# Attention with scores seven tiles ahead of the transposes instead of five, and weighted sums one behind instead of three

## The chip, the cores and the metric

The kernel runs on one core of a Trainium2 chip. The metric is the device time of one execution in microseconds (us), as the median of several runs. Profiles come from the hardware profiler, one execution each. Engines: PE multiplies matrices (PEld loads its weights), DVE is the vector engine, ACT evaluates functions and copies, POOL is the general engine, SP issues DMA transfers.

## The reference

One layer on a sequence of 2048 positions and a width of 1024: an input projection feeds two groups of eight heads of 64, an RWKV-7 recurrence and a stick-breaking attention; both are gated, put side by side, projected out and normalised. The change touches only the attention:

```
z      = q @ k.T / 8                        # 2048 x 2048 per head, strictly causal
log_1m = where(mask, log_sigmoid(-z), 0)
after  = cumsum from the right of log_1m, without the own element
attn   = where(mask, exp(log_sigmoid(z) + after), 0)
o      = attn @ v
```

So each weight is sigmoid(z) times the product of sigmoid(-z) over all later keys that are still before the query.

## The kernel before, in words

The program is one function, `trunk`. A first stage (0 to 132 us in the profile) makes the modulated input and its two half-precision parts; attention follows (132 to 1033 us); a second stage, with its own planner context, holds the recurrence and the output projection. The change is in the attention alone.

**Blocks and steps.** Attention goes through 16 blocks n = 4 j + b: four head pairs j, and in each four blocks of 512 queries b. Block b has 8 (b + 1) steps, so 8, 16, 24 and 32, in all 320; `seq` (L484 to L486) lists them. A step i of a block has three jobs, and i means another thing in each:

- `scores` (L495 to L526), for one tile of 128 queries and 512 keys: two matmuls into the PSUM tile `z` (L506, L507); ACT writes `u` = sigmoid(-z/8) (L510) and `s` = sigmoid(z/8) (L511); DVE runs a product scan over `u` from the last key to the first (L519 on the diagonal, L522 elsewhere), which starts from a column that POOL copies from the neighbouring tile (L521); POOL multiplies `s` by the scanned `u` (L523). Diagonal tiles are 128, 256, 384 and 512 wide. A group is four such tiles, for the four query tiles of one head and one block of keys.
- `turn` (L528 to L541), for 128 keys of a group: four PE transposes (L535), one from each `s` tile of the group, into the PSUM tile `tr`; ACT rounds it into `ah` (L539); DVE writes the rest `al` = tr - ah (L540).
- `weigh` (L543 to L566): two matmuls of `ah` and `al` with the values into the PSUM tile `av` (L553, L554); at the end of a head the result is copied out (L563, L564) and after the second head normalised and stored to DRAM (`finish`, L568).

**What is written down as order.** `attend` (L587 to L605) emits the jobs. Four constants rule it:

```
NS, NU, LEAD, LAG = 8, 5, 5, 3                                              # L481
...
        for p in range(p0, p1):
            if p + LEAD < min(p1 + ahead, len(seq)):
                yield scores(*seq[p + LEAD], sb)
            held.append(turn(*seq[p], sb))
            yield 0.43
            if len(held) > LAG:
                weigh(sb, *held.pop(0))
            yield 0.43
```

`ahead` is LEAD, but 0 in the blocks of 8 steps, whose successors' queries are not ready; the blocks of 16 steps begin with LEAD scores on their own (L592 to L594). `NS` and `NU` are the numbers of buffers of `s` and `u` (L508, L509), and LAG + 1 is that of `ah` and of `al` (L537, L538). `tr` has two PSUM buffers, `z` three, the projections' accumulator one and `av` one (L113, L127). `u` is also the buffer of a tile in the last projections of attention (L644).

**What fills the rest.** `fill` (L647) emits projections for later blocks, the splitting of weights into two half-precision parts and the combining of earlier results; a projection is 24 matmuls of 128x512 (L370 to L372). `_merge` (L712) interleaves `attend` and `fill` by shares of work.

**What sets the executed order.** The attention stage is planned with a timeline (`schedule_with_timeline_sim`, L109). The order of emission is a rank: the planner goes through a modelled time and gives each engine the instruction of highest rank whose inputs and buffers are ready. The order it ends with is fixed at compile time, and each engine then executes it in order, with semaphores between engines. In the last four blocks the first matmul of each accumulation of a projection is also held behind the newest weighted sum emitted so far (`pace`, L369, L555).

Of the kernel before, what the change touches and what calls it, by code (L numbers as in the profile page):

```python
# [88 lines left out]
def trunk(nc, a, out):  # L89
# [388 lines left out]
        V.scalar_tensor_tensor(out=sg, in0=tp, scalar=vec("sbg", 1, j), in1=sg, op0=ALU.mult, op1=ALU.mult)  # L478
        DMA.dma_start(out=ydram[4 + j][b], in_=sg)

    NS, NU, LEAD, LAG = 8, 5, 5, 3  # L481


    seq, steps = [], {}  # L484
# [851 lines left out]
```

## Time and profile before

| | |
|---|---|
| median of three runs (lowest to highest) | 1914.78 us (1912.62 to 1915.76) |
| the profiled execution's own time | 1910.53 us |
| its span in the trace | 1908.8 us |
| mean granted PE clock | 0.971 |
| attention, in the trace | 132 to 1033 us |

The profiled execution took 4.25 us less than the median of the three runs and 2.09 less than the lowest. Its span, the time between the first and the last instruction of the trace, is 1.7 us shorter than its time. "Busy" is time in which an engine worked; a bracket behind an instruction in a timeline is the engine's idle time before it and what ended it. A granted clock of 1.00 is 2.4 GHz, 0.50 is 1.2 GHz.

### The profile page before, as it was taken

How to read it: one execution, taken by the hardware profiler on the slowest of the kernel's cores; microseconds unless marked ns; L12 is line 12 of the kernel's file. 1: busy time of each engine (PE TensorE's matmuls, PEld its weight loads, DVE VectorE, ACT ScalarE, POOL GpSimd, SP SyncE). 2: the span in 40 equal slices, each digit the busy share in tenths (PEclk: the TensorE clock that was granted, in tenths of full speed). 3: DMA queues.
4: the chain of work that ended last, by engine and by line, in shares of the span. 5: the costliest groups of instructions: out<-in, count | busy, mean ns of one | idle time of the engine just before them, and what ended most of it. 6: DMA issues, size and time to landing. Idle time of an engine off the chain costs nothing. (4 is left out here: it accounts for less than half of the span.)

```text
span 1908.8 us, 38922 instructions
## 1 busy us (share of the span) xinstructions
PE 1719.8 (90%) x14880; PEld 1161.5 (61%) x14880; DVE 1348.7 (71%) x2855; ACT 870.0 (46%) x1718; POOL 754.6 (40%) x1106
## 2 busy tenths in 40 slices
PE   7979889999899998999997898898899888989998
PEld 2646556666566665667654455665555565667886
DVE  4876788577776778768775667877877777775542
ACT  2665567366654656546654333323332333422221
POOL 1425466355643646445444223222223232223322
PEclk9889999999999999999998899999999999999999
DMA  8442201222123221132111423222333333236442
GB/s 298 150 116 56 56 26 50 64 64 70 37 56 81 67 56 42 51 92 67 45 50 56 133 55 83 68 60 74 77 81 81 80 77 107 75 94 179 149 138 89
DMA packets 210408, 159.93 MB, mean 84 GB/s; under 512 B 113247, under 2 KB 171820, under 8 KB 210222
## 3 DMA queue, kind: packets, MB, share of 16 engines
q1 hardware_dynamic: 209220, 155.31, 29.2%
q8 instruction: 117, 1.92, 0.4%
q10 hardware_dynamic: 1002, 2.13, 0.4%
q14 instruction: 69, 0.57, 0.1%
HBM read 94.48 MB, written 44.04 MB: 73 GB/s over the span
## 5 line engine op out<-in xcount | busy, mean ns | idle before, releaser
L523 POOL TENSOR_TENSOR s<-s,u 128x512 f32<-128x512 f32 (+2 forms) x320 | 305.8, 963 | 216.5 <-ACT s L511 102.0
L540 DVE TENSOR_TENSOR al<-tr,ah 128x512 fp32r<-128x512 f32 (+1 forms) x320 | 187.4, 599 | 96.3 <-ACT ah L539 95.7
L522 DVE TENSOR_TENSOR_SCAN u<-u,dmask 128x512 f32<-128x512 f32 x192 | 240.0, 1268 | 13.0 <-ACT u L510 11.4
L539 ACT ACTIVATE ah<-tr 128x512 fp32r<-128x512 f32 (+1 forms) x320 | 171.7, 553 | 103.7 <-PE tr L535 99.6
L510 ACT ACTIVATE u<-z 128x512 f32<-128x512 f32 (+2 forms) x320 | 173.4, 555 | 73.4 <-PE z L507 49.0
L535 PE MATMUL tr<-kept_ident,s 128*128 128x128 f32 x1088 | 173.5, 279 | 33.1 <-DVE al L540 26.5
L511 ACT ACTIVATE s<-z 128x512 f32<-128x512 f32 (+2 forms) x320 | 166.2, 549 | 53.0 <-PE tr L535 53.0
L535 PEld LDWEIGHTS tr<-kept_ident,s 128*128 128x128 f32 x1088 | 130.3, 143 | 74.9 <-DVE al L540 38.4
L370 PE MATMUL pss<-kept_hh,kept_wh 128*128 128x512 f16 x416 | 161.3, 388 | 8.8 <-PEq L730 8.8
L372 PE MATMUL pss<-kept_hh,kept_wl 128*128 128x512 f16 x416 | 160.9, 387 | 0.0
L371 PE MATMUL pss<-kept_hl,kept_wh 128*128 128x512 f16 x416 | 160.9, 387 | 0.0
L372 PEld LDWEIGHTS <-kept_wl 128*128 128x128 f16 x928 | 93.2, 100 | 104.9 <-issue 14.2
L370 PEld LDWEIGHTS <-kept_wh 128*128 128x128 f16 x928 | 94.3, 102 | 101.4 <-issue 29.2
L371 PEld LDWEIGHTS <-kept_wh 128*128 128x128 f16 x928 | 93.0, 100 | 94.8 <-issue 25.0
L506 PE MATMUL z<-kt,qt 128*128 128x512 f32 (+2 forms) x320 | 132.1, 417 | 9.5 <-issue 3.7
L553 PE MATMUL av<-ah,vt 128*128 128x512 f32 (+1 forms) x320 | 136.5, 427 | 3.9 <-DVE o L564 2.3
L554 PE MATMUL av<-al,vt 128*128 128x512 f32 (+1 forms) x320 | 136.0, 426 | 0.2 <-DVE al L540 0.2
L507 PE MATMUL z<-kt,qt 128*128 128x512 f32 (+2 forms) x320 | 117.5, 371 | 0.0
L519 DVE TENSOR_TENSOR_SCAN u<-u,dmask 128x128 f32<-128x128 f32 (+3 forms) x128 | 107.3, 867 | 11.6 <-ACT u L510 6.6
L370 PE MATMUL psg<-kept_hh,kept_wh 128*128 128x512 f16 x256 | 99.1, 387 | 10.9 <-DVE klo L434 4.8
L1274 PE MATMUL po<-kept_woh,kept_yh 128*128 128x512 f32 x256 | 102.3, 400 | 0.0
L1275 PE MATMUL po<-kept_wol,kept_yh 128*128 128x512 f32 x256 | 101.5, 397 | 0.0
(296 smaller groups left out, 4146.1 us busy)
## 6 DMA issues: line engine op xcount, KB each, us to landing
kept_raw<-in_w_in SPq DMA_DIRECT2D x29, 512.0 KB, 4.3
ad<-in_ada_w SPq DMA_DIRECT2D x24, 512.0 KB, 5.6
qt<-qt SPq DMA_DIRECT2D x48, 256.0 KB, 3.3
xt<-in_x SPq DMA_DIRECT2D x16, 512.0 KB, 5.1
y<-sg SPq DMA_DIRECT2D x32, 256.0 KB, 2.3
t<-dt SPq DMA_DIRECT2D x64, 128.0 KB, 3.2
xr<-in_x SPq DMA_DIRECT2D x16, 512.0 KB, 3.6
out<-xr SPq DMA_DIRECT2D x16, 512.0 KB, 2.6
```

The source lines that it names most:

```text
L370: PE.matmul(ps, wh[:, k], hth[b][:, k], start=k == 0, stop=False)
L371: PE.matmul(ps, wh[:, k], htl[b][:, k], start=False, stop=False)
L372: PE.matmul(ps, wl[:, k], hth[b][:, k], start=False, stop=k == KB - 1)
L510: A.activation(out=u[:, 0:nk], in_=z[:, 0:nk], func=AF.Sigmoid, scale=-0.125)
L511: A.activation(out=s[:, 0:nk], in_=z[:, 0:nk], func=AF.Sigmoid, scale=0.125)
L522: V.tensor_tensor_scan(out=ur, data0=ur, data1=mr, initial=u[:, nk:nk + 1], op0=ALU.mult, op1=ALU.bypass)
L523: G.tensor_tensor(out=s[:, 0:nk], in0=s[:, 0:nk], in1=u[:, 1:nk + 1], op=ALU.mult)
L535: PE.transpose(tp[:, q * P:(q + 1) * P], att[gi, q][:, ks * P:(ks + 1) * P], ident)
L539: A.activation(out=ah[:, r], in_=tp[:, r], func=AF.Copy)
L540: V.tensor_tensor(out=al[:, r], in0=tp[:, r], in1=ah[:, r].bitcast(F32), op=ALU.subtract)
L553: PE.matmul(av[:, r], vs, ah[:, r], start=first, stop=False, skip_group_check=True)
L554: ins = PE.matmul(av[:, r], vs, al[:, r], start=False, stop=last, skip_group_check=True)
```

## The change

One line of constants changes.

```diff
-    NS, NU, LEAD, LAG = 8, 5, 5, 3
+    NS, NU, LEAD, LAG = 11, 6, 7, 1
```

`s` gets eleven buffers instead of eight and `u` six instead of five; `ah` and `al` get two instead of four each (LAG + 1). In bytes of a partition that is 3 x 2048 + 2052 more and 4 x 2048 less. Scores are emitted seven steps ahead of the turn that they stand beside, not five, and the blocks of 16 steps begin with seven scores; a weighted sum is emitted after the turn that follows its own, not after the third. No instruction is added or taken away.

## Rows read from the trace of the kernel before

**Rows 1.** The page, busy time of each engine over the span.
```profile
span 1908.8 us, 38922 instructions
...
PE 1719.8 (90%) x14880; PEld 1161.5 (61%) x14880; DVE 1348.7 (71%) x2855; ACT 870.0 (46%) x1718; POOL 754.6 (40%) x1106
```

**Rows 2.** Windows: stretch, its length, each engine's busy us, clock, DMA share, GB/s.
```profile
132.00:1033.00 901.00, 830.54 (x5338) 568.08 (x5338) 675.59 (x1001) 534.54 (x1122) 469.72 (x836) 0.98 0.21 56
...
580.00:609.00 29.00, 25.26 (x205) 17.81 (x204) 13.88 (x25) 11.20 (x25) 8.70 (x16) 1.00 0.37 92
609.00:656.00 47.00, 46.97 (x327) 32.56 (x326) 35.30 (x51) 27.98 (x62) 24.39 (x48) 1.00 0.25 68
...
717.00:808.00 91.00, 80.74 (x490) 55.18 (x490) 73.42 (x111) 54.13 (x112) 50.46 (x87) 0.96 0.17 49
```

**Rows 3.** Waits of PE, 132 to 1033: total us, times, longest.
```profile
PE tr L535 <- DVE al L540: 26.5, 27, 2.2
...
PE z L506 <- ACT s L511: 3.4, 4, 1.4
...
PE av L553 <- ACT ah L539: 1.3, 3, 0.9
```

**Rows 4.** Timeline, 773 to 778: start us, us, engine, line, operation.
```profile
773.61 0.63 ACT L539 ACTIVATE ah<-tr 128x512 fp32r<-128x512 f32 x1
...
773.76 1.27 DVE L522 TENSOR_TENSOR_SCAN u<-u,dmask 128x512 f32<-128x512 f32 x1
...
775.00 1.27 DVE L522 TENSOR_TENSOR_SCAN u<-u,dmask 128x512 f32<-128x512 f32 x1
...
776.23 0.68 DVE L540 TENSOR_TENSOR al<-tr,ah 128x512 fp32r<-128x512 f32 x1
...
776.96 0.66 PE L535 MATMUL tr<-kept_ident,s 128*128 128x128 f32 x4 [2.17 <-DVE al L540]
```

**Rows 5.** Groups by shape, 132 to 1033: busy us, mean ns, idle before.
```profile
L522 DVE TENSOR_TENSOR_SCAN u<-u,dmask 128x512 f32<-128x512 f32 x192 | 240.0, 1268 | 13.0 <-ACT u L510 11.4 <-POOL u L518 0.4
...
L540 DVE TENSOR_TENSOR al<-tr,ah 128x512 fp32r<-128x512 f32 x224 | 149.8, 679 | 80.3 <-ACT ah L539 80.0
...
L539 ACT ACTIVATE ah<-tr 128x512 fp32r<-128x512 f32 x224 | 135.9, 617 | 80.7 <-PE tr L535 76.8 <-DVE p L339 1.7 <-DVE al L540 0.7
...
L519 DVE TENSOR_TENSOR_SCAN u<-u,dmask 128x384 f32<-128x384 f32 x32 | 32.1, 1004 | 3.5 <-ACT u L510 3.5
```

**Rows 6.** Windows to 740.80 of single lines: L510, L511, L539, L554 (PE, PEld).
```profile
132.00:740.80 608.80, 121.37 (x223) 0.98 0.21 56
...
132.00:740.80 608.80, 114.16 (x220) 0.98 0.21 56
...
132.00:740.80 608.80, 115.10 (x215) 0.98 0.21 56
...
132.00:740.80 608.80, 90.40 (x213) 42.08 (x213) 0.98 0.21 56
```

**Rows 7.** Timelines of ACT and of DVE, 732 to 760.
```profile
741.14 1.58 ACT L511 ACTIVATE s<-z 128x512 f32<-128x512 f32 x3 [4.67 <-PE tr L535]
...
743.24 1.29 DVE L540 TENSOR_TENSOR al<-tr,ah 128x512 fp32r<-128x512 f32 x2 [5.79 <-ACT ah L539]
```

**Rows 8.** Windows, columns as in rows 2, of 736 to 756.
```profile
736.00:744.00 8.00, 7.69 (x42) 4.67 (x41) 2.21 (x5) 3.33 (x7) 2.18 (x3) 1.00 0.24 61
744.00:756.00 12.00, 9.54 (x57) 7.33 (x56) 11.93 (x20) 9.67 (x22) 9.20 (x18) 1.00 0.06 24
```

**Rows 9.** Waits of all engines, 132 to 1033, ACT's for transposes before `s`.
```profile
ACT s L511 <- PE tr L535: 53.0, 35, 4.7
```

**Rows 10.** Windows, columns as in rows 2, behind two of PE's waits.
```profile
724.00:728.00 4.00, 4.00 (x19) 3.37 (x18) 2.85 (x5) 2.55 (x5) 3.52 (x5) 0.68 0.00 0
...
776.00:780.00 4.00, 2.51 (x11) 1.90 (x12) 3.54 (x9) 1.29 (x3) 0.38 (x1) 0.72 0.01 4
780.00:784.00 4.00, 4.00 (x25) 3.35 (x24) 2.43 (x3) 3.72 (x8) 4.00 (x4) 0.86 0.00 0
```

## The prediction, made before the changed kernel ran

> **What bounds the kernel now.** I read the busy shares first: PE works 90% of the span (its weight loads beside that), DVE 71%, ACT and POOL under half [rows 1]. Then the windows by block, because the change touches only attention, 132 to 1033 us. There PE is busy 830.5 of 901 us, so 70.5 us of PE idle is nearly all that a new order can win [rows 2]. The reader is to see where it lies. A block of 16 steps (609 to 656) has PE busy 46.97 of 47 us. The block of 32 steps (717 to 808) leaves 10.3 us of 91 idle, with DVE busy 73.4 us, 81%. The block of 8 steps (580 to 609) leaves 3.7 of 29 idle, with DVE at 48%. So PE is the bound, and it loses time where DVE is full.
>
> Next the waits of PE in attention: the largest is the transposes waiting for the subtraction that writes `al`: 26.5 us in 27 waits, 0.98 us each [rows 3]. That subtraction is the last reader of the PSUM tile `tr`, of which there are two, so the transposes of step p need the `al` of step p-2. The timeline of one such wait shows why `al` is late: `ah` ended at 774.2, but DVE ran two scans of 1.27 us first, began `al` at 776.23, and PE stood still for 2.17 us [rows 4]. The subtraction takes only 0.68 us, a scan twice that [rows 5].
>
> Why do the scans come in a heap just then? By 740.80 the counts of instructions begun are 223 `u`, 220 `s`, 215 turns and 213 weighted sums [rows 6]. The next turn is number 215 (from 0), the last of the group 212 to 215, and all four tiles of a group are read by each of its four turns; so tiles 212 to 219 are held, eight, the whole ring. ACT stood for 4.67 us before the next `s`, until transposes had freed a group; DVE stood for 5.79 us before its next instruction [rows 7]. From 736 to 744 DVE is busy 2.21 us of 8, from 744 to 756 it is busy 11.93 of 12, and in that full stretch PE loses 2.46 us [rows 8]. In all of attention ACT waits 53.0 us in 35 waits for transposes before an `s` [rows 9]. So an idle DVE is followed by a full one, and the full one stops PE.
>
> **The change part by part.** It adds and removes no instruction: 320 scores, 320 turns, 320 weighted sums, all DMAs and every projection stay. It moves buffers (three `s` and one `u` more, two `ah` and two `al` fewer) and the rank at which each instruction is offered to the planner. Scores go two steps earlier, weighted sums two steps earlier against the turns. No DMA is issued by a moved score, and by a moved weighted sum only the store of a finished head pair on SP, 16 in all; no POOL queue is passed but by each score's own copy and product. So I cost these at nothing: a store runs beside the matmuls of the next step, and a late one would hold only the buffers of the next head's result, used once in 8 to 32 steps.
>
> *Eleven `s` instead of eight.* When ACT would stop at the eighth tile, three more scores can run, some 3 x 1.27 = 3.8 us of scans put into the hole of 5.79 us [rows 5, 7]. What remains late is the fourth score of a heap. Gain: between 0 and all of the 26.5 us of rows 3; a loss from buffers alone I exclude, because more of them only remove waits. I take half, 13.3 us, since the ring holds three scores of a heap of four but the planner may run ahead to the new limit and heap there again. The score matmul's own wait for ACT's `s`, 3.4 us in 4 waits [rows 3], has the same cause: half, 1.7 us, with 0 and 3.4 as ends. The sixth `u` goes with it at nothing.
>
> At this place a rule speaks against that term. The Trainium skill, Perfetto Trace Analysis, section Optimization Strategy, says that a bubble repeating on the engine that should be full can mean that SBUF or PSUM is short of room for the next tile. Read on the wait itself, that names the two `tr` tiles, which the change leaves at two, and the term would be 0 instead of 13.3 us, and the time that of no change.
>
> *The clock.* Behind two stalls the granted clock falls: 0.68 of full in 724 to 728, 0.72 and 0.86 in the 8 us from 776 [rows 10]. At 2.4 GHz as 1.00 and 1.2 as 0.50, the second costs 4 x 0.28 + 4 x 0.14 = 1.7 us of PE work. With half of the stalls gone I take two such falls less, 3.4 us; ends 0 and 7 (four falls, one for each block of 32).
>
> *Weighted sums one behind, two `ah` and `al`.* Program order puts the sum of step p-1 after the turn of p. A step is 91/32 = 2.84 us in the long blocks [rows 2]. From the start of a turn, `al` is there after 0.66 (transposes) + 0.62 (`ah`) + 0.68 = 1.96 us, 3.23 with one scan in front, 4.50 with two [rows 4, 5]. The sum's place is one step plus one turn later, 2.84 + 0.66 = 3.5 us, and some projection work beyond it. So with no scan or one it hides, and with two PE stands for up to a microsecond. Before, the place was two steps (5.7 us) further and nothing could reach it: the sums' wait for `ah` is 1.3 us in 3 waits [rows 3]. Not all is new, since the sums ran only two behind at 740.80 already [rows 6]. Bounds: 0, and as much as the transposes wait now, 26.5 us. I take a third of that, 9 waits of 0.98 us = 8.8 us, because two scans in front is the rarer case and a wait at the sum spares the next transposes the same one. Behind a waiting sum everything on PE is queued; behind an `ah` that waits for its buffer, ACT's next `u` and `s`.
>
> *Scores of the next head pair.* In a long block's tail seven of the next eight scores are made, not five. Three times two diagonal scans, each at most 1.00 us [rows 5], leave a block with DVE at 48% for one at 81% [rows 2]: at most 6 us, taken as 2.
>
> *Pacing.* In the last four blocks projection matmuls are held behind the newest weighted sum. That sum is now two steps newer, so less projection work is free to cover its wait. I count it in the 8.8 us and widen the upper end for it.
>
> Sum: -13.3 - 1.7 - 3.4 + 8.8 + 2 = -7.6 us. The profiled execution took 1910.5 us, 4.3 below the median of the three runs (1914.78) and 2.1 below their lowest. Against it the sum gives 1902.9; taken from the median, **1907.2 us**. A measurement of this kernel can tell about 0.2%, 3.8 us, from no change.
>
> **The rivals.**
> *Slower: PE waits at the weighted sums.* PE starts its matmuls in order; in rows 4 nothing started until `al` came. With two `ah` and two `al` a sum must be done before the `ah` of two steps later, so a late `al` now holds PE at the sum, the following turn and ACT. Place: the blocks of 24 and 32 steps, 224 of the 320. If one step in seven waits, that is 32 x 0.98 = 31 us, and three falls of the clock more, 5 us; less the gains of 18.4 and with the 2 us of scans it gives +20, 1935 us; at one in ten, 22 waits and no clock, +5, 1920 us. It decides from 17 such waits (16.4 us). For it: two of the three conditions (full DVE, two scans in a row) are in rows 4 and 8. Against: the place is a step and more away. The Trainium skill, TensorE: Matmul & The Clock Gate, section Step-by-step, says that matmuls keep program order and only weight loads are pulled ahead; the trace agrees, with 2.17 us in which no matmul started.
>
> *No change: the order is already there.* The planner offers an instruction when its inputs are ready, and rows 6 show scores eight ahead (by `u`) and sums two behind where the constants say five and three. If the planner runs to the ring's end again, the heaps are as large as now, and the `tr` tiles set the pace: 1914.8, within 3.8. Against it: the 5.79 us hole [rows 7] could take three scores more. The rule of the Trainium skill on bubbles (Perfetto Trace Analysis, Optimization Strategy) leads to this time too.
>
> **How the numbers follow.** Forecast (faster) 0.50, slower 0.30, no change 0.20. The forecast's own range is 1891 (three quarters of 26.5 + 3.4, that is 22.4, two falls, no new wait, 2 us of scans: -23.8) to 1911. All terms at their best ends together (-26.5 - 3.4 - 7) would be 1878, which I leave out. To leave no more than 2 in 10 out in all, I reach down to 1890 and up into the slower case as far as 1927, between its two prices. Faster by over 0.2% 0.50, within 0.20, slower 0.30.
>
> **What would show it.** Right: ACT's wait for transposes before an `s` well under 53 us, the counts of rows 6 at ten or eleven `u` ahead of the turns, DVE without stretches like 744 to 756, transposes waiting for `al` near 13 us, PE busier in the blocks of 32. Wrong: a new row of weighted sums waiting for `al` or `ah` over 16 us (slower), or transposes waiting for `al` at 26 us as before (no change). The stage behind 1033 us should be the same to the microsecond; a difference there would be a fault of my reading.

## The result and the profile after

The changed kernel takes **1932.11 us** (median of 5 runs, 1930.01 to 1939.69) against 1915.75 (median of 5 runs, 1912.62 to 1920.50) before: ratio 1.0097, 95% interval [1.0069, 1.0126]. It is slower by 0.97%, outside the predicted range and on the other side of it. The profiled execution took 1930.01 us.

The page first, its busy shares, to be set beside [rows 1]:

```profile
span 1928.3 us, 38969 instructions
...
PE 1729.7 (90%) x14880; PEld 1166.6 (61%) x14880; DVE 1352.3 (70%) x2855; ACT 870.2 (45%) x1718; POOL 747.6 (39%) x1106
```

The shares have not moved by more than a point, so they say nothing of the cause. The span is 19.5 us longer. The windows show where, with the columns of [rows 2]; the blocks of 8, 16 and 32 steps there are 580 to 609, 609 to 656 and 717 to 808 before, and stand here 5 to 9 us later. Two windows of the kernel before come first, the last four blocks of attention and what follows attention:

```profile
1036.00:1908.80 872.80, 780.98 (x8955) 536.05 (x8954) 582.31 (x1650) 271.14 (x500) 251.26 (x229) 0.97 0.35 95
808.00:1036.00 228.00, 212.97 (x1328) 142.27 (x1326) 167.48 (x261) 132.17 (x269) 110.89 (x185) 0.99 0.21 58
```

and the kernel after:

```profile
585.00:613.00 28.00, 24.88 (x205) 17.49 (x203) 14.79 (x31) 11.43 (x25) 8.83 (x16) 1.00 0.42 109
613.00:662.00 49.00, 48.64 (x330) 33.00 (x329) 38.18 (x50) 31.59 (x69) 28.19 (x54) 1.00 0.21 57
724.00:817.00 93.00, 82.08 (x487) 56.29 (x486) 68.49 (x104) 50.88 (x107) 46.64 (x80) 0.94 0.17 48
817.00:1053.00 236.00, 213.16 (x1322) 141.34 (x1321) 169.85 (x265) 132.70 (x268) 111.01 (x185) 0.99 0.20 56
1053.00:1928.30 875.30, 782.49 (x8960) 538.39 (x8958) 583.84 (x1651) 271.58 (x501) 250.13 (x229) 0.97 0.35 95
```

From the start of the first score matmul to the start of the last transpose of L572 attention took 906.1 us before and 923.2 after, 17.1 of the 19.5 us. The last four blocks alone are 8 us longer (228 to 236) with PE busy for as long (212.97, 213.16): that part is standing still.

PE's waits in 130 to 1060 (columns as in [rows 3]) say what it stood still for:

```profile
PE otp L572 <- DVE o L564: 22.5, 8, 4.2
PE av L554 <- DVE al L540: 19.5, 23, 2.7
PE av L553 <- ACT ah L539: 5.8, 11, 1.4
PE z L506 <- ACT s L511: 4.8, 10, 1.4
...
PE tr L535 <- DVE al L540: 1.0, 2, 0.7
```

and of the kernel before, the same view:

```profile
PE otp L572 <- DVE o L564: 5.1, 4, 1.4
...
PE av L553 <- ACT ah L539: 1.3, 3, 0.9
PE av L554 <- DVE al L540: 0.2, 1, 0.2
```

The wait that the change aimed at, the transposes' for `al`, is all but gone: 26.5 us [rows 3] became 1.0. The same late `al` now stops PE one place earlier, at the second matmul of the weighted sum: that and the wait for `ah` are 25.3 us in 34 waits, 1.5 us in 4 before. On top of it stands a row that the prediction did not speak of, L572, the transposes that finish a head pair: 22.5 us, 17.4 more than before.

The timeline of one wait at a sum (columns as in [rows 4]):

```profile
784.49 0.60 PE L535 MATMUL tr<-kept_ident,s 128*128 128x128 f32 x4
...
784.74 1.27 DVE L522 TENSOR_TENSOR_SCAN u<-u,dmask 128x512 f32<-128x512 f32 x1
...
784.99 0.49 PE L553 MATMUL av<-ah,vt 128*128 128x512 f32 x1
785.93 0.45 DVE L519 TENSOR_TENSOR_SCAN u<-u,dmask 128x128 f32<-128x128 f32 x1
786.35 0.68 DVE L540 TENSOR_TENSOR al<-tr,ah 128x512 fp32r<-128x512 f32 x1
...
787.08 0.59 PE L554 MATMUL av<-al,vt 128*128 128x512 f32 x1 [1.60 <-DVE al L540]
```

It is the picture of [rows 4] with another victim. The next turn's transposes (784.49) come straight before the sum, so PE has 1.0 us of work left (784.49 to 785.48) while DVE puts a full and a narrow scan ahead of `al`, and then it stands for 1.60 us.

The timeline of one wait at L572, where a block of 32 steps begins; the same wait of 4.0 to 4.2 us stands there for each of the four head pairs:

```profile
726.54 0.40 PE L507 MATMUL z<-kt,qt 128*128 128x512 f32 x1
...
726.66 0.59 ACT L563 ACTIVATE olo<-av 64x512 f32<-64x512 f32 x1
...
727.43 0.98 DVE L346 TENSOR_SCALAR rkw<-kept_his,ws 128x8 f32<-128x8 f32 x1
...
728.33 1.27 DVE L522 TENSOR_TENSOR_SCAN u<-u,dmask 128x512 f32<-128x512 f32 x1
...
729.52 0.66 DVE L540 TENSOR_TENSOR al<-tr,ah 128x512 fp32r<-128x512 f32 x1
730.21 0.68 DVE L564 TENSOR_TENSOR o<-av,olo 64x512 f32<-64x512 f32 x1
...
730.95 1.12 PE L572 MATMUL otp<-kept_ident,o 128*128 128x128 f32 x4 [4.01 <-DVE o L564]
```

The finish needs a copy on ACT (L563) and an addition on DVE (L564) behind the last sum. The copy ends at 727.25; DVE first does an operation of 0.98 us on weights (L346), a scan and an `al`, and adds at 730.21. Before, the sum was emitted two turns later and the finish with it; by 723.20 PE had waited 1.45 us at the same place.

What a stall costs afterwards can be read from the granted clock (windows of 4 us, columns as in [rows 2], clock third from the end):

```profile
728.00:732.00 4.00, 1.05 (x5) 1.06 (x6) 3.94 (x5) 0.37 (x1) 2.51 (x4) 0.67 0.00 0
732.00:736.00 4.00, 4.00 (x16) 3.43 (x15) 3.22 (x6) 3.66 (x8) 3.21 (x5) 0.50 0.00 0
```

PE worked 1.05 us of four, and the next four ran at 0.50, the 1.2 GHz level.

### The profile page after: what moved, and what is told of

The parts are those of the page before. It is cut to its first block, busy times and chain, and to the rows that moved or that the text cites. A ratio compares the mean times of both kernels' runs of the same rounds, so it can differ in the third digit from the quotient of the medians.

```text
span 1928.3 us, 38969 instructions
## 1 busy us (share of the span) xinstructions
PE 1729.7 (90%) x14880; PEld 1166.6 (61%) x14880; DVE 1352.3 (70%) x2855; ACT 870.2 (45%) x1718; POOL 747.6 (39%) x1106
## 5 line engine op out<-in xcount | busy, mean ns | idle before, releaser
L522 DVE TENSOR_TENSOR_SCAN u<-u,dmask 128x512 f32<-128x512 f32 x192 | 238.8, 1266 | 22.6 <-ACT u L510 22.2
L539 ACT ACTIVATE ah<-tr 128x512 fp32r<-128x512 f32 (+1 forms) x320 | 173.6, 554 | 137.9 <-PE tr L535 109.7
L510 ACT ACTIVATE u<-z 128x512 f32<-128x512 f32 (+2 forms) x320 | 174.7, 566 | 52.1 <-PE z L507 35.9
L511 ACT ACTIVATE s<-z 128x512 f32<-128x512 f32 (+2 forms) x320 | 169.1, 555 | 45.0 <-PE tr L535 44.7
L535 PE MATMUL tr<-kept_ident,s 128*128 128x128 f32 x1088 | 178.4, 280 | 7.5 <-ACT otok L574 3.4
L535 PEld LDWEIGHTS tr<-kept_ident,s 128*128 128x128 f32 x1088 | 136.8, 144 | 38.8 <-ACT otok L574 5.4
L554 PE MATMUL av<-al,vt 128*128 128x512 f32 (+1 forms) x320 | 134.9, 422 | 20.0 <-DVE al L540 19.5
L553 PE MATMUL av<-ah,vt 128*128 128x512 f32 (+1 forms) x320 | 143.7, 449 | 8.1 <-ACT ah L539 5.8
L506 PE MATMUL z<-kt,qt 128*128 128x512 f32 (+2 forms) x320 | 140.1, 441 | 7.7 <-ACT s L511 4.8
L507 PE MATMUL z<-kt,qt 128*128 128x512 f32 (+2 forms) x320 | 118.7, 374 | 0.0
L347 POOL TENSOR_TENSOR kept_raw<-kept_raw,rkw 128x1024 f32<-128x1024 f32 x29 | 55.3, 1908 | 127.0 <-DVE rkw L346 107.5
```

The source lines that it names most:

```text
L510: A.activation(out=u[:, 0:nk], in_=z[:, 0:nk], func=AF.Sigmoid, scale=-0.125)
L511: A.activation(out=s[:, 0:nk], in_=z[:, 0:nk], func=AF.Sigmoid, scale=0.125)
L522: V.tensor_tensor_scan(out=ur, data0=ur, data1=mr, initial=u[:, nk:nk + 1], op0=ALU.mult, op1=ALU.bypass)
L535: PE.transpose(tp[:, q * P:(q + 1) * P], att[gi, q][:, ks * P:(ks + 1) * P], ident)
L539: A.activation(out=ah[:, r], in_=tp[:, r], func=AF.Copy)
```

## The experiments

Eighteen kernels. All are edits of the kernel before unless said otherwise; where `bufs=LAG + 1` is replaced for `ah` (L537), it is for `al` (L538) too. "Attention" is the length from the start of the first score matmul to the start of the last transpose of L572 in the profiled execution; it was 906.1 us before. Ratios are to the kernel before on the same chip, with the 95% interval.

| run | NS, NU, LEAD, LAG; ah and al each | median us (runs) | ratio | attention us |
|---|---|---|---|---|
| after | 11, 6, 7, 1; 2 | 1932.11 (5) | 1.0097 [1.0069, 1.0126] | 923.2 |
| e1_rank1 | 8, 5, 5, 1; 4 | 1938.44 (4) | 1.0113 [1.0057, 1.0168] | 929.4 |
| e12_lag1_buf2 | 8, 5, 5, 1; 2 | 1935.46 (4) | 1.0083 [1.0054, 1.0111] | 926.0 |
| e2_buf2 | 8, 5, 5, 3; 2 | 1928.23 (10) | 1.0056 [1.0035, 1.0078] | 915.0 |
| e17_buf3 | 8, 5, 5, 3; 3 | 1920.20 (10) | 1.0013 [0.9986, 1.0040] | 915.2 |
| e4_lead7 | 11, 6, 7, 3; 2 | 1946.78 (4) | 1.0141 [1.0091, 1.0191] | 939.1 |
| e11_s11_lead5 | 11, 6, 5, 3; 2 | 1939.69 (4) | 1.0103 [1.0078, 1.0128] | 933.8 |
| e10_lead7_s8 | 8, 5, 7, 3; 4 | 1913.87 (10) | 0.9970 [0.9944, 0.9995] | 903.2 |
| e16_s10_buf3 | 10, 5, 5, 3; 3 | 1908.82 (10) | 0.9970 [0.9942, 0.9999] | 895.7 |
| e5_finish_late | after, finish later | 1940.75 (4) | 1.0115 [1.0073, 1.0157] | 929.7 |
| e9_after_pace | after, pace held back | 1931.26 (6) | 1.0074 [1.0038, 1.0110] | 920.8 |
| e6_share_up | before, other share | 1914.47 (8) | 0.9991 [0.9970, 1.0013] | 902.2 |
| e7_share_down | before, other share | 1920.90 (8) | 1.0028 [1.0006, 1.0050] | 912.5 |
| e8_after_share_up | after, other share | 1936.42 (2) | 1.0115 [1.0067, 1.0164] | 923.7 |
| e19_lag4 | 8, 5, 5, 4; 4 | 1918.03 (12) | 1.0005 [0.9987, 1.0022] | 905.3 |
| e13_lag5 | 8, 5, 5, 5; 4 | 1902.80 (4) | 0.9916 [0.9894, 0.9939] | 894.9 |
| e14_lag6 | 8, 5, 5, 6; 4 | 1913.55 (10) | 0.9980 [0.9960, 1.0001] | 902.0 |
| e15_lead7_lag5 | 8, 5, 7, 5; 4 | 1906.29 (10) | 0.9954 [0.9933, 0.9975] | 892.8 |
| e18_s10_lag5 | 10, 5, 5, 5; 3 | 1908.19 (6) | 0.9947 [0.9927, 0.9967] | 898.0 |

### Which part of the change costs: the rank of the sums alone

```diff
-    NS, NU, LEAD, LAG = 8, 5, 5, 3
+    NS, NU, LEAD, LAG = 8, 5, 5, 1
...
-        ah = sb.tile([P, TB], F32R, tag="ah", bufs=LAG + 1, name="ah")
+        ah = sb.tile([P, TB], F32R, tag="ah", bufs=4, name="ah")
```

> The kernel before with LAG 1 alone in rank, its four buffers each of ah and al kept (NS, NU, LEAD stay 8, 5, 5). Theory R (the weighted sums' rank costs the time: PE is given them, and the transposes of a finished head pair, as soon as the plan thinks their inputs ready, and stands there on the chip): 1926 to 1936 us, at least 15 us of PE's waits in attention at L553, L554 and L572, transposes waiting for al under 10 us. Theory S (seven scores ahead and eleven s cost it): as before, 1912 to 1920. Theory B (two ah and al buffers instead of four cost it): as before, 1912 to 1920.

Ratio 1.0113 [1.0057, 1.0168]. Weighted sums one behind, with every buffer as before, cost as much as the whole change. PE's waits (130 to 1060) are those of the changed kernel:

```profile
PE otp L572 <- DVE o L564: 25.3, 10, 3.7
PE av L554 <- DVE al L540: 21.0, 27, 1.9
PE av L553 <- ACT ah L539: 9.1, 9, 2.5
```

The same rank with two `ah` and `al`, the change without its scores (the LAG line as above, no line for `ah`):

> The kernel before with LAG 1 as the change has it, rank and two buffers each of ah and al; scores as before (8, 5, 5). Theory R (the rank of the weighted sums is what costs): as the run with the rank alone, attention 924 to 935 us, 1930 to 1942, so that the change's score side gives some 6 us back. If rank and buffers add up: attention 933 to 945, 1940 to 1955.

1.0083 [1.0054, 1.0111], the same within the intervals. With sums one behind the missing buffers cost nothing that can be told: ACT's wait for a weighted sum before an `ah` is 5.1 us.

### The buffers alone, and the change without the rank

```diff
-        ah = sb.tile([P, TB], F32R, tag="ah", bufs=LAG + 1, name="ah")
+        ah = sb.tile([P, TB], F32R, tag="ah", bufs=2, name="ah")
```

> The kernel before with two buffers each of ah and al instead of four, all four constants as before (8, 5, 5, 3). Theory R: as before, 1910 to 1920 us, since the weighted sums ran two behind anyway and the rank is unchanged. Theory S: as before. Theory B: 1926 to 1936, with ah waiting for weighted sums on ACT and PE's waits in attention up by 10 us or more.

1.0056 [1.0035, 1.0078]. With sums three behind, two buffers do cost. ACT's waits in this run show the place:

```profile
ACT s L511 <- PE tr L535: 26.0, 23, 4.3
ACT ah L539 <- PE av L553: 22.7, 12, 4.2
```

ACT stands for weighted sums to free an `ah`. It no longer stands so long for `s` (53.0 before, [rows 9]), but that buys nothing. The time is the one that theory B named, so the buffers have a price of their own; but PE's idle time in attention did not grow (68.7 us against 72.3), so how ACT's wait becomes time is not shown.

```diff
-    NS, NU, LEAD, LAG = 8, 5, 5, 3
+    NS, NU, LEAD, LAG = 11, 6, 7, 3
...
-        ah = sb.tile([P, TB], F32R, tag="ah", bufs=LAG + 1, name="ah")
+        ah = sb.tile([P, TB], F32R, tag="ah", bufs=2, name="ah")
```

> The kernel after (11, 6, 7) with LAG 3 in rank and two buffers each of ah and al as in after. Theory R: the loss is gone, 1900 to 1918 us; L572 waits under 6 us in attention, and if the score side gains what was predicted for it, 1900 to 1910. Theory S: 1926 to 1936, nothing gained. Theory B: 1926 to 1936.

1.0141 [1.0091, 1.0191], the slowest of all and slower than any of the three theories had it: the change without its rank is no better than with it. So the rank alone is enough for the loss, and taking the rank back does not cure it. Eleven `s` with four `ah` and `al` would need 8196 bytes of a partition more than the kernel before, and the program has fewer than 2048 left, so the score half was not tried with its own buffers alone. The parts do not add: rank +1.1%, rest +1.4%, both +1.0%.

### The wait at L572, and the pacing

The changed kernel with the finish of a head pair emitted two steps after its last sum (its lines below L487 stand one lower):

```diff
+    later = []
...
-                finish(n, avs["o"], sb)
+                later.append([2, n, avs["o"]])
...
+            for it in list(later):
+                it[0] -= 1
+                if it[0] < 0:
+                    later.remove(it)
+                    finish(it[1], it[2], sb)
...
```

> The kernel after, with the finish of a head pair (the four transposes L572 and what follows them) emitted two steps later than the last weighted sum instead of at once. Theory R in the part for L572 (22.5 us of PE's waits in after against 5.1 before): 1912 to 1924 us, L572 waits under 8 us, the waits at L553 and L554 (25 us) as in after. If the L572 waits are hidden by something else that takes their place (theories S and B): 1928 to 1936.

1.0115 [1.0073, 1.0157]: nothing came back, where 1912 to 1924 us had been expected. The waits at the finish are gone, 22.5 us of them, and PE's list (130 to 1060) now has

```profile
PE av L555 <- DVE al L541: 18.4, 19, 2.6
PE tr L536 <- DVE al L541: 10.6, 12, 1.6
```

so part of it went back to the transposes, and the granted clock was below 1 for 54.6 us of attention instead of 41.0. PE's idle time in attention fell only from 78.5 to 73.7 us, and its busy time grew by more. A wait in a list is not a time to be had.

The changed kernel with the projections of the last four blocks held behind the sum two older:

```diff
-    held = []
+    held, paced = [], []
...
-            pace[0] = ins.ins
+            paced.append(ins.ins)
+            pace[0] = paced[max(0, len(paced) - 3)]
```

> The kernel after with the projections of the last four blocks held behind the weighted sum two older than the newest, which is where three behind put them. Theory P (the hold is too tight with sums one behind: the last four blocks took 236.2 us in after, from 817.3 to 1053.5, against 227.7 before): these blocks 226 to 231 us, 1922 to 1928 us in all. Theories R and L: these blocks not shorter by more than 3 us, 1928 to 1940.

1.0074 [1.0038, 1.0110]; the last four blocks took 233.0 us instead of 236.2 (227.7 before, all three from the block's first turn to the last transpose). Pacing is worth some 3 of their 8.5 us; the runs do not tell it from nothing in the total.

### Is it luck of the plan

A planner can turn any small edit into another order. Attention's share in the interleaving was moved by 1% either way, in the kernel before and in the changed one:

```diff
-            _merge((attend(n, sb), 8.6 + 10.48 * b), (fill(n, sb), fill_work(n)))
+            _merge((attend(n, sb), 8.6 + 10.6 * b), (fill(n, sb), fill_work(n)))
```

> The kernel before with a neutral change to the plan alone: attention's share in the interleaving with the projections is 8.6 + 10.6 b instead of 8.6 + 10.48 b; all four constants as before. Theory L (the order before is a lucky one, and nearly any new plan stands 8 to 30 us worse, whatever it was meant to do): 1923 to 1945 us, with PE's waits in attention at the transposes for al or elsewhere. Theory R (the weighted sums' rank): 1910 to 1922, attention within 8 us of the 905.9 us of before.

With 10.36 in place of 10.6:

> The kernel before with the other neutral change, 8.6 + 10.36 b; all four constants as before. Theory L: 1923 to 1945 us. Theory R: 1910 to 1922.

The changed kernel with 10.6:

> The kernel after with the neutral change 8.6 + 10.6 b. Theory L: as likely better as worse than after, anywhere from 1918 to 1948 us, and a different list of PE's longest waits. Theory R: 1926 to 1938, with L572 waits near 22 us and weighted sums waiting for al near 20 us as in after.

0.9991, 1.0028 and 1.0115. Edits that mean nothing move the kernel before by up to 0.3%, and stand 0.4% apart; one did not bring the changed kernel back, and its waits at the sums and the finish were there again. Luck of the plan does not make the +1%, which all six kernels with sums one behind show (1.0074 to 1.0115). A difference of 0.3% between two plans it can make.

### The score half

```diff
-    NS, NU, LEAD, LAG = 8, 5, 5, 3
+    NS, NU, LEAD, LAG = 8, 5, 7, 3
...
-        ah = sb.tile([P, TB], F32R, tag="ah", bufs=LAG + 1, name="ah")
+        ah = sb.tile([P, TB], F32R, tag="ah", bufs=4, name="ah")
```

> The kernel before with LEAD 7 in rank alone; eight s, five u, three behind, four ah and al as before. Theory D (scores ranked two steps earlier put scans ahead of the subtraction al on DVE, and the transposes wait longer): attention 918 to 940 us against 905.9, the transposes' wait for al on PE 30 us or more, 1926 to 1946 us in all. Theory Q (the eleven s, not the rank, let DVE heap scans in front of al): attention within 8 us of before, 1908 to 1922 us.

0.9970 [0.9944, 0.9995]: scores seven ahead are free, or a slight gain no larger than luck of the plan. The eight `s` hold them back: at a turn's start `u` was 6.84 steps ahead on average, 6.54 before.

```diff
-    NS, NU, LEAD, LAG = 8, 5, 5, 3
+    NS, NU, LEAD, LAG = 11, 6, 5, 3
...
-        ah = sb.tile([P, TB], F32R, tag="ah", bufs=LAG + 1, name="ah")
+        ah = sb.tile([P, TB], F32R, tag="ah", bufs=2, name="ah")
```

> The kernel before with eleven s and six u, five ahead and three behind in rank as before, and two buffers each of ah and al (four do not fit beside eleven s); to be held against the run with two buffers alone (attention 915.0 us, transposes waiting 23.4 us for al). Theory D: attention 910 to 920, waits for al as there or less, 1918 to 1930 us. Theory Q: attention 925 to 940, waits for al 30 us or more, 1934 to 1950 us. The prediction on record (the ring's room takes half of those waits away): waits for al 10 to 14 us, attention 900 to 908, 1910 to 1920.

1.0103 [1.0078, 1.0128], slower than two `ah` and `al` alone (1.0056). PE's waits here:

```profile
PE tr L535 <- DVE al L540: 34.1, 43, 2.7
PE z L506 <- ACT s L511: 11.4, 14, 1.4
```

and ACT's:

```profile
ACT ah L539 <- PE av L553: 29.3, 15, 4.9
ACT s L511 <- PE tr L535: 14.0, 12, 3.5
```

Eleven `s` did cut ACT's wait for transposes before an `s`, to 14.0 us (26.0 in e2_buf2). Both waits that this was to relieve grew instead: transposes for `al` 34.1 us (22.6 in e2_buf2), scores for `s` 11.4 us.

To see more `s` with less shortage elsewhere, three `ah` and `al`, first without and then with ten `s`:

```diff
-        ah = sb.tile([P, TB], F32R, tag="ah", bufs=LAG + 1, name="ah")
+        ah = sb.tile([P, TB], F32R, tag="ah", bufs=3, name="ah")
```

> The kernel before with three buffers each of ah and al instead of four; all else as before (8, 5, 5, 3). Control for the next. Sums run two behind in the executed order, so three buffers hold what is alive: attention 900 to 913 us against 905.9, 1908 to 1922 in all. If even the third is short: attention 912 to 920.

```diff
-    NS, NU, LEAD, LAG = 8, 5, 5, 3
+    NS, NU, LEAD, LAG = 10, 5, 5, 3
...
-        ah = sb.tile([P, TB], F32R, tag="ah", bufs=LAG + 1, name="ah")
+        ah = sb.tile([P, TB], F32R, tag="ah", bufs=3, name="ah")
```

> The kernel before with ten s instead of eight, paid for by three buffers each of ah and al (10, 5, 5, 3). Theory Q (more s by themselves cost, since the plan runs scans further ahead of al): attention 10 us or more above the run with three buffers and eight s, the transposes' wait for al 30 us or more. Theory A (eleven s cost only because ACT's u and s stand behind an ah that waits for one of its two buffers): attention within 6 us of that run, waits for al 22 to 28 us. The prediction on record: attention 5 to 13 us below it, waits for al near 13 us.

1.0013 [0.9986, 1.0040] and 0.9970 [0.9942, 0.9999], on one chip. So the kernel with two more `s` is 11.4 us faster beside three `ah` (1920.20 to 1908.82), close to the term of the sum, yet not where the sum looked for it: the transposes' wait for `al` rose from 24.6 to 29.5 us. In the two profiles the time below full clock in attention fell, 54.6 to 27.3 us, at half speed up to 13.7 us of matmuls. But over the ten runs of each the mean granted clock is 0.972 against 0.969, some 4 us of the span, so the two profiles overstate it. The cause of the 11.4 us stays open, and two neutral plans of the kernel before differ by 6.4 us.

### The other way: sums later

If early sums cost, late ones should not. Four `ah` and `al` in each:

```diff
-    NS, NU, LEAD, LAG = 8, 5, 5, 3
+    NS, NU, LEAD, LAG = 8, 5, 5, 5
...
-        ah = sb.tile([P, TB], F32R, tag="ah", bufs=LAG + 1, name="ah")
+        ah = sb.tile([P, TB], F32R, tag="ah", bufs=4, name="ah")
```

> The kernel before with weighted sums five behind in rank instead of three, with four buffers each of ah and al as before. Theory R, carried on: later in rank costs nothing or gains, attention 895 to 910 us, 1900 to 1920, with weighted sums not waiting for ah or al at all. If three behind is a balance: attention 912 or more, with the wait moved to ah's buffers on ACT.

0.9916 [0.9894, 0.9939], **1902.80 us, the best kernel here, faster than both**. PE's waits:

```profile
PE tr L535 <- DVE al L540: 28.3, 29, 2.5
...
PE otp L572 <- DVE o L564: 0.7, 1, 0.7
...
PE av L554 <- DVE al L540: 0.2, 1, 0.2
```

The finish no longer waits (5.1 before, 0.7), the transposes wait as before, and attention has 27.3 us below full clock instead of 37.5. All PE idle time in attention went from 72.3 to 64.2 us. The mean granted clock of its four runs is 0.973, against 0.967 of the thirteen runs of the kernel before beside them, some 12 us of the span, so a good part of the gain of 16 us goes with the clock; the runs do not part clock and waits. With LAG 4 and 6 in the first line of that diff:

> The kernel before with weighted sums four behind in rank, four buffers each of ah and al. Theory R as a smooth curve: between three and five behind, 1903 to 1914 us. If five behind is only one good plan among others: anywhere in 1903 to 1925, above 1916 as likely as below.

> The kernel before with weighted sums six behind in rank, four buffers each of ah and al. Theory R: the executed order can't be more than four behind, and was 2.04 behind with five; nothing more to gain: attention 890 to 902 us, 1897 to 1910. If the sums, held back further, begin to block ah on ACT: attention 905 or more.

1.0005 [0.9987, 1.0022] and 0.9980 [0.9960, 1.0001]. The curve over LAG is 1: +1.1%, 3: 0, 4: 0, 5: -0.8%, 6: -0.2%: a loss on the early side, nearly flat on the late one, with five as one good plan among them. Two behind was not run. The wait at the finish is 0.7 us with four and six behind too, so its going is not what makes five faster. Why five and not four or six stays open.

Five with scores seven ahead (8, 5, 7, 5), and five with ten `s` and three `ah` and `al` (10, 5, 5, 5):

> The kernel before with scores seven ahead and sums five behind, buffers as before (8 s, 5 u, 4 ah, 4 al). If the two ranks act each by itself (-3 and -11 us of attention): attention 885 to 899 us, 1893 to 1908 in all. If the rank of the scores is nothing: as the run with sums five behind, 890 to 900.

> Ten s, five u, three buffers each of ah and al, scores five ahead, weighted sums five behind (10, 5, 5, 5). If room for s and late sums add up (-0.3% and -0.8%): 1890 to 1900 us. If both reach the same waits: 1898 to 1912. If three buffers are short for sums five behind in rank: 1912 to 1930.

0.9954 and 0.9947: both keep a gain, neither adds to it.

## Why the prediction was wrong

**The step that failed** is the part "Weighted sums one behind", in its sentence that a step is 2.84 us and the sum's place 3.5 us from the start of its turn, so that "with no scan or one it hides". 2.84 us is a mean. In the changed kernel's trace turns start 2.85 us apart on average, but 155 of the 319 spacings are under 2 us (151 before): turns come in heaps like scores do, with projection work between the heaps. In 51 steps the second matmul of a sum began within 0.1 us of the end of its `al` (before, in the very last step alone), and in 44 of those the next turn had begun under 2 us after its own. In the timeline at 784 the sum's first matmul stood 0.5 us after that next turn. The chain to `al` was priced well: from a turn's first transpose to the end of its `al` the trace has 1.96 us in the lowest tenth and a median of 2.85. A chain with a median of 2.85 cannot hide behind a place that is under 2.7 us away (a short spacing and a turn of 0.66) in half of the cases: it is the longer of the two in 143 of the 319 steps. With the spacings of the trace before it would have been 161, so this could have been read beforehand. Other PE work covered most of them. Priced at 9 waits and 8.8 us, the term took 34 waits and 25.3 us.

**What the prediction left out** is the finish. A finished head pair was costed only as a store on SP; that its transposes are PE work at a sum's rank, behind an ACT copy and a DVE addition, was not seen, though a row for it, 4.3 us in 3 waits, was in the view of [rows 3]. It came to 17.4 us more. Yet e5_finish_late shows that this row was not a price by itself: without it the time was the same.

**Eleven `s`, -13.3 us.** The exclusion "a loss from buffers alone I exclude" is right for buffers added, and the trade took others away. By the counts of the changed kernel to 750 us (columns and lines as in [rows 6])

```profile
132.00:750.00 618.00, 122.68 (x226) 0.98 0.21 55
...
132.00:750.00 618.00, 118.03 (x224) 0.98 0.21 55
...
132.00:750.00 618.00, 115.77 (x215) 0.98 0.21 55
...
132.00:750.00 618.00, 91.37 (x214) 42.06 (x215) 0.98 0.21 55
```

`u` is 11 ahead of the turns and the sums one behind, both as forecast. But ACT's wait before an `s` only fell from 53.0 us [rows 9] to

```profile
ACT s L511 <- PE tr L535: 44.7, 31, 5.0
```

and DVE kept its full stretches, against 11.93 of 12 us in [rows 8]:

```profile
756.00:772.00 16.00, 14.61 (x76) 9.37 (x76) 15.69 (x23) 12.00 (x23) 11.97 (x16) 1.00 0.12 34
```

So the planner ran to the new limit and heaped there, the half that the prediction had set against the term. In no run with ten or eleven `s` and sums three or five behind was the transposes' wait for `al` shorter than before (29.5 to 35.1 us in the four of them, 26.5 in [rows 3]). In the changed kernel it fell to 1.0 us, as it did with eight `s` in e1_rank1 and e12_lag1_buf2 (1.0 us in each), so it is the rank that moved it: a PE that has waited at the sum does not wait again at the turn. The Trainium skill's rule in the prediction (Perfetto Trace Analysis, Optimization Strategy), read on the two `tr` tiles, gave 0 for this term. The waits of the four runs agree with that reading, but three `tr` tiles were not tried.

**The clock, -3.4 us.** Nothing was saved: attention was below full clock for 37.5 us before and 41.0 after. A fall stands at each of the four stalls of 4 us (265, 497, 729 and 968 us), where before two falls stood (494 and 723). The slowdown itself is not the clock's: the two profiled executions have the same mean, 0.971.

**Scores for `s`, -1.7 us:** 3.4 [rows 3] became 4.8. **Pacing:** about 3 us in one profile, counted inside the 8.8 and not told from nothing in the total. **Scores of the next head pair, +2:** no run tells it apart.

**What follows attention** was to be "the same to the microsecond": 872.8 before, 875.3 after. That was too strict; the eighteen runs, which leave this code alone, have 869 to 883 us there.

**The slower rival** was right in the mechanism and in the place: 27 of the 34 waits lie in the blocks of 24 and 32 steps, and its deciding point of 17 waits was passed twice over. That its worked case, 32 waits and 1935 us, lies so near to the 1932 us is in part luck: the waits at the sums came to 25.3 us and not 31, the three falls of the clock (5 us) hardly came, and the finish and the longer busy time, which came, were in none of its terms. It was given 0.30 because of "the place is a step and more away", the same mean step.

**How the 17.1 us of attention are made up.** By the list of waits: at the sums +23.8 (1.5 to 25.3), at the finish +17.4, at the transposes -25.5, and smaller ones, -9.5 together; all PE idle time rose only by 6.2 (72.3 to 78.5). The other 10.8 are busy time, 833.7 to 844.5 us for the same matmuls. In the first three head pairs these groups (columns as in [rows 5]) are before

```profile
L553 PE MATMUL av<-ah,vt 128*128 128x512 f32 x239 | 100.6, 422 | 1.1 <-DVE o L564 0.7 <-ACT ah L539 0.2
L506 PE MATMUL z<-kt,qt 128*128 128x512 f32 x245 | 100.3, 414 | 6.8 <-ACT s L511 2.9 <-DMA qt<-qt 1.9 <-issue 1.8
```

and after

```profile
L506 PE MATMUL z<-kt,qt 128*128 128x512 f32 x245 | 107.6, 441 | 7.0 <-ACT s L511 4.8 <-DMA qt<-qt 1.1
L553 PE MATMUL av<-ah,vt 128*128 128x512 f32 x239 | 106.4, 445 | 4.9 <-ACT ah L539 3.4 <-DVE o L564 1.4
```

The first matmul of a score and of a sum is recorded 23 to 27 ns longer, 13 us in all (records overlap, so this need not add up with the 10.8). 3.5 us more below full clock can make some 2 of that. Most of the rest, about 10 us, goes with what stands just ahead on PE. A matmul of 512 columns is recorded some 0.48 us long directly behind a turn's transposes and 0.40 behind another score or sum, here in the trace before:

```profile
746.62 0.66 PE L535 MATMUL tr<-kept_ident,s 128*128 128x128 f32 x4 [0.52 <-DVE mx L336]
747.03 0.47 PE L553 MATMUL av<-ah,vt 128*128 128x512 f32 x1
...
751.14 0.40 PE L507 MATMUL z<-kt,qt 128*128 128x512 f32 x1
751.37 0.40 PE L553 MATMUL av<-ah,vt 128*128 128x512 f32 x1
```

Directly behind transposes stood the first matmul of a sum in 48 of 320 steps before and in 138 after, that of a score in 25 and in 85. The rank does it: in the six kernels with sums one behind it is 126 to 140 sums and 79 to 94 scores, in all others 22 to 52 and 22 to 58. How much of the longer records is time that PE lost is not shown.

**Shown and open.** Shown: the rank of the sums alone is enough for the slowdown, with the same waits (e1_rank1, e12_lag1_buf2); sums five behind gain in three kernels (e13_lag5, e15_lead7_lag5, e18_s10_lag5); neutral plans move 0.3%. The other half of the change costs as much alone when it has two `ah` and `al` (e4_lead7). Not shown: that the listed waits, one by one, make up the loss, since taking away those at the finish gave nothing back. Open: why eleven `s` with two `ah` and `al` are worse than eight, why rank and rest together cost no more than either, and why LAG 5 beats 4 and 6.

## What to carry to other kernels

In a stream that one engine executes in order, place the consumer of a chain through other engines by the short spacings of its neighbours, not by their mean: here steps came in heaps, and half of the spacings were well under the mean. When a wait is to be removed, ask which instruction on the same engine will meet the same late producer next, and follow all that hangs on the moved step (here the finish of a head pair) to its own wait. Buffers and ranks are one setting: two `ah` and `al` cost 0.56% with sums three behind and nothing measurable with one behind, so measure them together and test the opposite direction of a change too.

## What was not expected of the hardware

The code after attention, untouched, took 869 to 883 us over the profiles, so a difference of ten microseconds between two single profiles cannot be read as an effect; medians were needed. The granted clock goes with it: the shortest (e13_lag5) was below full clock there for 37.6 us, the longest (e18_s10_lag5) for 64.7. The same holds for whole executions of one program: among 31 of the kernel before on one chip the fastest, 1905.79 us, had a mean clock of 0.974, and the slowest, 1925.05 us, had 0.962. And recorded PE busy time is not fixed work: the same 14880 matmuls were busy 1719.8 us before [rows 1], 1729.7 after and 1743.2 in e5_finish_late; part of that goes with the order, as the records behind transposes show.
